# Two gate projections issued in the last attention job of a hybrid decoder layer, in place of jobs 8 to 10

## The chip, the core and the metric

The kernel runs on one NeuronCore of a Trainium2 chip. The core has five engines with an instruction stream each: TensorE (PE, matrix products into PSUM), VectorE (DVE), ScalarE (ACT), GpSimd (POOL) and SyncE (SP, which issues most DMA transfers). Each stream is worked off in its written order, and semaphores tie the streams together. The metric is the time of one execution on the device in microseconds (us), the median of the runs shown.

## The reference

One layer over 1024 tokens of width 1024. The normalised input is projected into four head groups of width 512, each of which also has a gate path; their outputs are normalised per head, gated, concatenated and projected back:

```python
h = rms_norm(h_res, norm_gain[l])
proj = h @ w_in[l]
(aq, ak, av, ag, bq, bk, bv, bg, cq, ck, cv, cg, cf, d_in, dg) = _split(proj, IN_WIDTHS)
...
oa = from_heads(differential_attention(qa, ka, va, bias_by_dist, lam))
...
ob = from_heads(stick_breaking_attention(...))
...
oc = from_heads(forgetting_attention(qc, kc, to_heads(cv, H_C, HEAD_DIM), log_f))
...
od = rwkv7_branch(d_in, rwkv_mu[l], ...)
mixed = jnp.concatenate([oa * jax.nn.silu(ag), ob * jax.nn.silu(bg),
                         oc * jax.nn.silu(cg), od * jax.nn.silu(dg)], axis=-1)
h_res = h_res + mixed @ w_out[l]
```

Group A is differential attention (4 heads), B stick-breaking attention (8 heads), C forgetting attention (8 heads), D an RWKV-7 state recurrence (8 heads). A gate here means silu of 128 columns of `ag`, `bg`, `cg` or `dg` for all tokens.

## The kernel before

The mixed width of 2048 is cut into 16 feature blocks f of 128: 0 to 3 are group A, 4 to 7 B, 8 to 11 C, 12 to 15 D. A projection (`proj`, L271) of 128 columns is 48 matmuls `pj` on L280: two token halves, eight slices of the contraction, three terms each (high and low parts of weights and activations). Its weights are loaded by two SP transfers and split by POOL into `wh` (L191) and `wl` (L192), 4 instructions. The activations `hTh` and `hTl` stay in SBUF until the last projection; `hp.close()` (L1143) gives their place to the tiles of the recurrence.

The attention runs as 12 jobs: 0 to 3 are pairs of heads of B, 4 to 7 heads of A, 8 to 11 pairs of heads of C. A job of C makes score tiles `sc` (L414, L418) on PE, a bias tile `bt` and a normalisation on POOL (L630, L631, L634), minima on DVE (L565), exponentials on ACT (L570); then `pv` (L426) transposes the weights (`pt`, L434), splits them into `pth` (ACT, L437) and `ptl` (DVE, L438) and multiplies them with the values (`po`, L443 and L444), four times 16 to 32 `po` rows for a job (8, 8, 16 and 16 pairs by halves and heads). While job i is in attention, the q, k and v projections of job i+1 are issued, and behind them the gate projections that the table `FILL` names for job i: `proj_gate_exp` (L397), whose evacuation of each half is a copy, three exponential or logarithm passes on ACT (L400, L402, L659, L660), one DVE (L658) and one POOL instruction (L404), and a store into `gates`. A scheduler places the instructions of each engine by priority and dependences; `hold` ties the first matmul of a gate that `FILL` names for job 11 behind that job's first score (L281).

A block f of `otb` or of a job is finished by `finish` (L456): loads of the attention output and the gate, a square on ACT (L294), a matmul `psn` of ones (L295) into a PSUM bank of one buffer, Ln and Exp on ACT (L238, L241), one DVE and one POOL product, and a store into `mix`. `FIN` names the blocks finished during a job, `LASTF` those finished behind the attention, after the two halves that job 11 has `held`.

Behind the last projection stands the recurrence of D, 16 chunks of 64 tokens: `chunk_local` and `chunk_state` (L991, L1018), each chunk six groups `psf` of matmuls (L986) with DVE steps between and a state step `pss` of 64 rows in the trace (L1040 to L1049); every second chunk is normalised (`pmean` L1063, `pvar` L1069). The output weights are split in 16 steps by `split_w` (L881): an SP load `wraw` into one of two buffers, a cast `woh` on ACT (L886, L891), a difference `wol` on POOL (L887, L892). The first eight use tiles that the attention frees, the other eight tiles that are free behind it. The output projection `pso` (L949) begins with three groups of feature blocks (4,5), (6,7), (8,9), runs then beside chunks of the recurrence, and takes blocks in the order of `WORDER`, (0,1), (10,11) and (2,3) next.

Of the kernel before, what the change touches and what calls it, by code (L numbers as in the profile page):

```python
# [41 lines left out]
SB = 1  # L42
EXP_LN_SET = 6
LATE_A = 4
FILL = {0: [4], 1: [5], 2: [6], 3: [7], 7: [8], 8: [9, 0, 1], 9: [10, 2], 10: [11, 3], 11: []}
FIN = {4: [4], 5: [5], 6: [6], 7: [7], 8: [0], 9: [1], 10: [2]}
OHW = 1152
NAV = 2
TMPB = 5
# [9 lines left out]
CUT2 = 4  # L59
EARLYG = 3  # L60
WFIRST = False
LASTF = (3,)


def shape_constants():
# [25 lines left out]
def hybrid_trunk_kernel(  # L91
# [296 lines left out]
    def proj_gate(f, tmp):  # L388
        def evac(hf, cs, ps):
            e = tmp.tile([P, HS], F32, tag="pjt", bufs=2, name="ge")  # L390
            sigmoid(e, ps)
            nc.vector.tensor_mul(e, ps, e)
            nc.sync.dma_start(gates[f, :, cs], e)

        proj(COL["abcd"[f // 4] + "g"] + f % 4 * P, evac)

    def proj_gate_exp(f, hold=None):  # L397
        def evac(hf, cs, ps):
            g = at.cbp.tile([P, HS], F32, tag="gg", bufs=2, name="gg")
            nc.scalar.copy(g, ps)  # L400
            e = at.cbp.tile([P, HS], F32, tag="ge", bufs=2, name="gx")
            nc.scalar.activation(e, g, AF.Exp, scale=-1.0)  # L402
            sigmoid_of(e)
            nc.gpsimd.tensor_mul(e, g, e)  # L404
            nc.sync.dma_start(gates[f, :, cs], e)

        proj(COL["abcd"[f // 4] + "g"] + f % 4 * P, evac, hold=hold)
# [48 lines left out]
    def finish(ot, f, J, sumw, width, tmp):  # L456
        cs = slice(J * HS, (J + 1) * HS)
        gt = at.fin.tile([P, HS], F32, tag="gl", bufs=2, name="gl")
        nc.sync.dma_start(gt, gates[f, :, cs])
        rs = head_rstd(ot, sumw, width, at.fin.tile([P, HS], F32, tag="tmp", bufs=TMPB, name="sq"), bank("av", 1, "psn"))  # L460
        y = at.fin.tile([P, HS], F32, tag="tmp", bufs=TMPB, name="y")
        nc.vector.scalar_tensor_tensor(y, ot, og[:, f:f + 1], rs, op0=ALU.mult, op1=ALU.mult)
        nc.gpsimd.tensor_mul(y, y, gt)
        nc.sync.dma_start(mix[f * P:f * P + P, cs], y)
# [79 lines left out]
    def proj_head_a(p, pl, tmp, late=None):  # L544
        t = qk_tiles(pl)
        proj_qk(COL["aq"] + p * P, "q", t, qkg[:, 0:1], tmp, late)
        proj_qk(COL["ak"] + p * P, "k", t, qkg[:, 1:2], tmp, late)
        t["v"] = proj_v(COL["av"] + p * P, pl, tmp, 1)
        tb = pl.tile([P, S], F32, tag="bt", bufs=2, name="tb")
        base = at.skew[p]  # L550
        src = bass.AP(base.tensor, base.offset + P - 1, [[OHW - 1, P], [1, S]])
        nc.sync.dma_start(tb, src)
        t["tb"] = tb
        return t
# [543 lines left out]
    with ExitStack() as st:  # L1098
# [9 lines left out]
        for i, (pf, af, j) in enumerate(jobs):  # L1108
# [6 lines left out]
            if i == 3:  # L1115
                late = []
                nxt = proj_head_a(0, pl, tmp, late)
                for f in FILL[i]:
                    proj_gate(f, tmp)
# [5 lines left out]
            if i < 3:  # L1125
                for f in FILL[i]:
                    proj_gate(f, tmp)
# [3 lines left out]
            elif i >= 7:  # L1131
                for f in FILL[i]:
                    proj_gate_exp(f, at.first if i in HOLD else None)
            for f in FIN.get(i, []):
                for J in range(2):
# [30 lines left out]
        for h in at.held:  # L1166
            finish(*h)
        for f in LASTF:
            for J in range(2):
# [42 lines left out]
```

## Time and profile before

| | |
|---|---|
| median of 3 runs | 1561.72 us (1561.05 to 1561.87) |
| the profiled execution | 1562.11 us, of which 1560.3 us are the span of its instructions |
| PE busy | 94% of the span, 8180 matmuls |
| DVE, ACT, POOL busy | 64%, 47%, 58% |
| granted TensorE clock | 0.984 of full speed |

The profile shows one execution. An engine's busy time is the time in which it had an instruction in work; a matmul's end is modelled and neighbours overlap in the pipeline, so a stream of matmuls that never pauses is priced by the step from one start to the next. The PE, PEld, DVE, ACT and POOL columns are busy times, with the number of instructions in brackets.

### The profile page before, as it was taken

The numbers are of one execution on the slowest core, as the hardware profiler recorded it, in microseconds if no ns is written. First come the engines' busy times: TensorE is split into PE (matmuls) and PEld (weight loads), VectorE is DVE, ScalarE is ACT, GpSimd is POOL, SyncE is SP. The second block draws the span as 40 slices with busy tenths as digits, with TensorE's granted clock in tenths as the row PEclk, the third lists the DMA queues.
The fourth block names the chain that finished last, engine by engine and source line by source line (L and its number), as shares of the span: only waits on it lengthen the run. The fifth ranks groups of instructions, "written<-read, shape, count | busy, mean of one in ns | idle before, by whom it ended". The sixth has DMA issues, their size and how long they took to land.

```text
span 1560.3 us, 23517 instructions
## 1 busy us (share of the span) xinstructions
PE 1465.9 (94%) x8180; PEld 1180.1 (76%) x8180; DVE 999.8 (64%) x1763; ACT 739.8 (47%) x1602; POOL 911.6 (58%) x999
## 2 busy tenths in 40 slices
PE   7899999988889898889999999999999999999998
PEld 4677777766667676668887878878877777888887
DVE  6677865488988877676677664463558774444321
ACT  5534343344444443475666665665566654211110
POOL 3566755899999999513334367767678745100000
PEclk9999999999999999989999999999999999999999
DMA  6444557321213131542233333324339547465231
GB/s 159 107 109 118 131 149 217 84 55 54 68 34 82 48 109 41 128 129 62 78 92 88 82 105 118 106 84 128 87 97 220 156 113 233 117 161 124 77 115 61
DMA packets 259759, 168.77 MB, mean 108 GB/s; under 512 B 127948, under 2 KB 222412, under 8 KB 259512
## 3 DMA queue, kind: packets, MB, share of 16 engines
q1 hardware_dynamic: 259640, 167.26, 40.1%
q8 instruction: 65, 1.06, 0.3%
q14 instruction: 54, 0.44, 0.1%
HBM read 107.40 MB, written 49.60 MB: 101 GB/s over the span
## 4 chain that ended last, share of the span: by engine, by line
PE 58%; POOL 20%; DVE 8%; issue 6%; ACT 3%; DMA 2%; SPq 1%; POOLq 0%; DVEq 0%; ACTq 0%
PE pj L280 25%; PE pso L949 10%; POOL yinv L874 7%; POOL ytmp L872 6%; PE psf L986 5%; POOL wl L192 3%; PE pt L434 3%; PE psn L295 3%; PE sc L414 2%; PE sc L418 2%; PE po L444 1%; PE po L443 1%; DMA wraw<-in_w_out_dram 1%; POOL wh L191 1%; POOL sh L699 1%
## 5 line engine op out<-in xcount | busy, mean ns | idle before, releaser
L280 PE MATMUL pj<-hTh,wh 128*128 128x512 f32 (+1 forms) x1040 | 423.2, 407 | 30.5 <-POOL wh L191 15.6
L280 PE MATMUL pj<-hTh,wl 128*128 128x512 f32 (+1 forms) x1040 | 417.9, 406 | 20.0 <-POOL wl L192 18.0
L280 PE MATMUL pj<-hTl,wh 128*128 128x512 f32 (+1 forms) x1040 | 416.1, 401 | 0.8 <-DVE hTl L268 0.8
L280 PEld LDWEIGHTS pj<-hTh,wh 128*128 128x128 f32 (+1 forms) x1040 | 199.0, 191 | 83.3 <-POOL wh L191 23.9
L280 PEld LDWEIGHTS pj<-hTh,wl 128*128 128x128 f32 (+1 forms) x1040 | 198.7, 191 | 70.8 <-POOL wl L192 24.5
L280 PEld LDWEIGHTS pj<-hTl,wh 128*128 128x128 f32 (+1 forms) x1040 | 198.8, 191 | 42.9 <-issue 3.0
L192 POOL TENSOR_TENSOR wl<-raw,wh 128x512 fp32r<-128x512 f32 (+1 forms) x130 | 183.4, 1411 | 8.4 <-PE pj L280 3.0
L191 POOL TENSOR_SCALAR wh<-raw 128x512 fp32r<-128x512 f32 (+1 forms) x130 | 99.1, 762 | 130.3 <-PE pj L280 106.3
L437 ACT CAST pth<-pt 128x512 fp32r<-128x512 f32 x240 | 107.9, 482 | 102.0 <-PE pt L434 96.4
L438 DVE TENSOR_TENSOR ptl<-pt,pth 128x512 fp32r<-128x512 f32 x240 | 125.4, 548 | 33.8 <-ACT pth L437 32.7
L492 DVE TENSOR_TENSOR_SCAN qs<-qs 128x128 f32<-128x128 f32 (+3 forms) x96 | 135.3, 1413 | 10.9 <-ACT qs L138 10.7
L570 ACT ACTIVATE Pt<-Pt,st 128x512 f32<-128x512 f32 (+2 forms) x192 | 117.0, 612 | 49.5 <-DVE st L565 45.2
L874 POOL TENSOR_TENSOR yinv<-yinv,ytmp 128x486 f32<-128x486 f32 (+44 forms) x106 | 129.6, 1222 | 4.1
L494 DVE TENSOR_TENSOR Pt<-Pt,qs 128x128 f32<-128x128 f32 (+3 forms) x96 | 102.3, 1068 | 38.7 <-POOL qs L491 17.1
L872 POOL TENSOR_TENSOR ytmp<-yinv 128x486 f32<-128x486 f32 (+44 forms) x106 | 117.7, 1111 | 8.1 <-DMA yinv<-mab 4.5
L1079 POOL TENSOR_TENSOR yc<-yc,lbg 128x512 f32<-128x512 f32 x16 | 20.8, 1298 | 164.6 <-DVE yc L1073 132.6
L434 PE MATMUL pt<-cst,Pt 128*128 128x128 f32 x720 | 115.0, 275 | 0.8 <-DVE Pt L494 0.5
L414 PE MATMUL sc<-k,q 128*128 128x512 f32 (+3 forms) x288 | 111.8, 389 | 3.7 <-DVE st L565 3.0
L434 PEld LDWEIGHTS pt<-cst,Pt 128*128 128x128 f32 x720 | 86.8, 141 | 17.7 <-issue 3.4
L418 PE MATMUL sc<-k,ql 128*128 128x512 f32 (+3 forms) x288 | 99.3, 349 | 0.0
L138 ACT ACTIVATE qs<-sc 128x128 f32<-128x128 f32 (+3 forms) x96 | 47.8, 498 | 89.9 <-DVE qs L492 42.5
L949 PE MATMUL pso<-wol,omh 128*128 128x512 f32 x224 | 89.1, 398 | 0.0
(255 smaller groups left out, 2961.7 us busy)
## 6 DMA issues: line engine op xcount, KB each, us to landing
raw<-in_w_in_dram SPq DMA_DIRECT2D x128, 256.0 KB, 3.0
cb<-cum SPq DMA_DIRECT2D x16, 512.0 KB, 4.2
bd<-abky SPq DMA_DIRECT2D x32, 256.0 KB, 4.9
wraw<-in_w_out_dram SPq DMA_DIRECT2D x16, 512.0 KB, 4.1
om<-mix SPq DMA_DIRECT2D x32, 256.0 KB, 3.1
q<-q SPq DMA_DIRECT2D x48, 128.0 KB, 2.3
k<-kl SPq DMA_DIRECT2D x48, 128.0 KB, 2.3
gl<-gates SPq DMA_DIRECT2D x24, 256.0 KB, 2.9
```

Of the source, the lines that this page charges most:

```text
L191: nc.gpsimd.tensor_scalar(wh[:, :, :M], raw[:, :, :M], 1.0, 0.0, op0=ALU.mult, op1=ALU.add)
L192: nc.gpsimd.tensor_sub(wl[:, :, :M], raw[:, :, :M], wh[:, :, :M].bitcast(F32))
L280: mm = nc.tensor.matmul(pss[hf][:M, :], lhsT=a[:, kt % 4, :M], rhs=b[:, kt, cs], start=n == 0, stop=n == 3 * KT - 1)
L414: mm = nc.tensor.matmul(ps[:, :w], lhsT=t[f"q{h}"][qh][:, qs], rhs=t[f"k{h}"][:, c0:c1], start=True, stop=False)
L418: nc.tensor.matmul(ps[:, :w], lhsT=t[f"l{h}"][qh][:, qs], rhs=t[f"k{h}"][:, c0:c1], start=False, stop=not diag)
L434: nc.tensor.transpose(pt[:, (b - a) * P:(b - a + 1) * P], ptiles[b][kb // 4][:, kb % 4 * P:(kb % 4 + 1) * P], ident)
L438: nc.vector.tensor_sub(pl[:, :n], pt[:, :n], ph[:, :n].bitcast(F32))
L492: nc.vector.tensor_tensor_scan(q[:, :w][:, ::-1], q[:, :w][:, ::-1], q[:, :w][:, ::-1], 1.0 if after is None else after, op0=ALU.mult, op1 ...
L570: nc.scalar.activation(et[:, :w], et[:, :w], AF.Exp, scale=-1.0, bias=init, accum_out=st[:, 2 + i:3 + i])
L872: nc.gpsimd.tensor_mul(t, y[:, a:a + n, r:r + 1].to_broadcast([P, n, r]), y[:, r:r + 1, :r].to_broadcast([P, n, r]))
L874: nc.gpsimd.tensor_add(y[:, a:a + n, :r], y[:, a:a + n, :r], t)
L949: mm = nc.tensor.matmul(ps[b][half], lhsT=l, rhs=r[half], start=n == 0, stop=n == 47)
```

## The change

Three tables are changed. Block 1 is projected as a gate in job 9 and no longer in job 8; blocks 2 and 3 move from jobs 9 and 10 to job 11, where `hold` puts them behind the first score. Block 2 is finished behind the attention, with block 3, and no longer in job 10.

```diff
-FILL = {0: [4], 1: [5], 2: [6], 3: [7], 7: [8], 8: [9, 0, 1], 9: [10, 2], 10: [11, 3], 11: []}
-FIN = {4: [4], 5: [5], 6: [6], 7: [7], 8: [0], 9: [1], 10: [2]}
+FILL = {0: [4], 1: [5], 2: [6], 3: [7], 7: [8], 8: [9, 0], 9: [10, 1], 10: [11], 11: [2, 3]}
+FIN = {4: [4], 5: [5], 6: [6], 7: [7], 8: [0], 9: [1]}
...
-LASTF = (3,)
+LASTF = (2, 3)
```

On PE, before the change, the rows around the first `po` of job 10 (bank `po_11055`, keys `k1_10558`); `pj_11906` is the second half of the last gate, block 3:

```order
L280 MATMUL pj_11906<-hTh_140,wh_11901 128x512
L280 MATMUL pj_11906<-hTl_141,wh_11901 128x512
L280 MATMUL pj_11906<-hTh_140,wl_11902 128x512
L443 MATMUL po_11055<-pth_11061,vs_10735 128x512
L444 MATMUL po_11055<-ptl_11062,vs_10735 128x512
L443 MATMUL po_11055<-pth_11071,vs_10735 128x384
L444 MATMUL po_11055<-ptl_11072,vs_10735 128x384
L443 MATMUL po_11055<-pth_11080,vs_10735 128x256
L444 MATMUL po_11055<-ptl_11081,vs_10735 128x256
```

With the change, the last scores of job 10 (keys `k1_10478`), its first long `po` bank, the first score of job 11 (keys `k0_11474`) and what follows; `pj_12347` is the first half of the gate of block 2:

```order
L414 MATMUL sc_11356<-k1_10478,q1_10476 128x512
L418 MATMUL sc_11356<-k1_10478,ql1_2400 128x512
L414 MATMUL sc_11361<-k1_10478,q1_10476 128x512
L418 MATMUL sc_11361<-k1_10478,ql1_2400 128x512
L443 MATMUL po_11204<-pth_11210,vs_10655 128x512
L444 MATMUL po_11204<-ptl_11211,vs_10655 128x512
L443 MATMUL po_11204<-pth_11221,vs_10655 128x512
L444 MATMUL po_11204<-ptl_11222,vs_10655 128x512
L414 MATMUL sc_11820<-k0_11474,q0_11470 128x128
L418 MATMUL sc_11820<-k0_11474,ql0_2396 128x128
L280 MATMUL pj_12347<-hTh_140,wh_12337 128x512
L280 MATMUL pj_12347<-hTl_141,wh_12337 128x512
```

Before, all projections are through when job 10's first `po` bank starts, and no matmul of a projection follows; now the first gate of the two begins some 80 rows behind the last matmul of block 11's gate, two thirds into job 10, and the rows between hold none. The first rows of the recurrence, which need the place of `hTh` and `hTl`, move behind the second gate.

On ACT, behind the attention, before the change: the casts of the last output weights (12 to 15), and the square (L294), Ln (L238) and Exp (L241) of the finishes; `psn_13088` and `psn_13100` belong to the first and second:

```order
L886 CAST woh12_14273<-wraw_14275 128x1024
L238 ACTIVATE sq_13087<-psn_13088,epst_129 128x512
L241 ACTIVATE sq_13087<-sq_13087 128x512
L294 ACTIVATE sq_13099<-ot_12186 128x512
L886 CAST woh13_14279<-wraw_14281 128x1024
L1011 COPY bdm0_12533<-psf_13251 64x4x64
L238 ACTIVATE sq_13099<-psn_13100,epst_129 128x512
L886 CAST woh14_14285<-wraw_14287 128x1024
```

The same place with the change; the first and second finish are `psn_13060` and `psn_13072`:

```order
L886 CAST woh12_14273<-wraw_14275 128x1024
L886 CAST woh13_14279<-wraw_14281 128x1024
L238 ACTIVATE sq_12887<-pvar_12889,epst_129 128x512
L241 ACTIVATE sq_12887<-sq_12887 128x512
L886 CAST woh14_14285<-wraw_14287 128x1024
L238 ACTIVATE sq_13059<-psn_13060,epst_129 128x512
L241 ACTIVATE sq_13059<-sq_13059 128x512
L886 CAST woh15_14291<-wraw_14293 128x1024
L294 ACTIVATE sq_13071<-ot_11998 128x512
L238 ACTIVATE sq_13071<-psn_13072,epst_129 128x512
```

The square of the second finish stood ahead of the cast of block 13 and stands now behind that of block 15, the last. Six finishes stand behind the attention and not four.

On PE, behind the attention with the change, the rows from the last of the first three output groups to the second finish; `pss_13191` is the state step of chunk 4, which before the change ran beside job 11's last `po` bank:

```order
L949 MATMUL pso_12966<-woh9_12946,oml_13030 128x512
L295 MATMUL psn_13060<-sq_13059,cst_65 128x512
L986 MATMUL psf_13144<-cR_12816,bd0_12503 128x128 x4
L986 MATMUL psf_13155<-rkv1_12513,bd1_12509 128x128 x4
L986 MATMUL psf_13162<-cR_12816,bdm0_12505 128x128 x4
L295 MATMUL psn_13072<-sq_13071,cst_65 128x512
L986 MATMUL psf_13168<-rkv1_12513,bd1_12509 128x128 x4
L986 MATMUL psf_13177<-cR_12816,bdm0_12505 128x128 x4
L986 MATMUL psf_13184<-rkv1_12513,bd1_12509 128x128 x4
L1040 MATMUL pss_13191<-cS_12880,cQ_13182 64x64
```

Everything behind the second `psn`, chunk 4 included, waits for it on PE; from the state step of chunk 7 on, the order of PE is that of before.

## Rows read from the trace of the kernel before

**Rows 1.** Busy time by stretch; after the engines: granted clock, DMA share, GB/s.

```profile
1069.20:1169.20 100.00, 99.18 (x481) 80.68 (x480) 51.10 (x122) 61.93 (x137) 69.49 (x88) 1.00 0.31 96
1169.20:1234.90 65.70, 60.43 (x438) 47.64 (x436) 53.76 (x135) 47.19 (x112) 56.89 (x72) 1.00 0.74 185
1234.90:1279.90 45.00, 43.07 (x380) 35.14 (x382) 35.46 (x78) 23.34 (x55) 20.18 (x20) 1.00 0.52 141
1279.90:1340.80 60.90, 58.18 (x456) 47.77 (x456) 30.23 (x42) 25.99 (x41) 29.43 (x15) 1.00 0.69 197
1340.80:1560.30 219.50, 215.46 (x1599) 182.01 (x1598) 75.69 (x132) 33.51 (x63) 13.09 (x10) 1.00 0.40 107
```

**Rows 2.** By stretch, the projections (L280) alone: PE, PEld, clock, DMA share, GB/s.

```profile
1069.20:1169.20 100.00, 72.64 (x289) 53.37 (x288) 1.00 0.31 96
```

**Rows 3.** By stretch, the recurrence's `psf` groups (L986) alone, same columns.

```profile
1169.20:1234.90 65.70, 21.66 (x160) 20.04 (x160) 1.00 0.74 185
1234.90:1279.90 45.00, 14.05 (x104) 13.00 (x104) 1.00 0.52 141
1279.90:1340.80 60.90, 19.01 (x144) 17.53 (x144) 1.00 0.69 197
```

**Rows 4.** Timeline of PE: start, duration; gate matmuls, finishes, recurrence.

```profile
1168.60 0.39 PE L280 MATMUL pj<-hTh,wh 128*128 128x512 f32 x1
1168.83 0.39 PE L280 MATMUL pj<-hTl,wh 128*128 128x512 f32 x1
...
1299.63 1.02 PE L295 MATMUL psn<-sq,cst 128*128 128x512 f32 x2
1300.49 1.05 PE L986 MATMUL psf<-cR,bdm 128*128 128x128 f32 x8
1301.38 1.06 PE L986 MATMUL psf<-rkv,bd 128*128 128x128 f32 x8
...
1303.32 1.02 PE L295 MATMUL psn<-sq,cst 128*128 128x512 f32 x2
...
1306.19 0.34 PE L1040 MATMUL pss<-cS,cQ 64*64 64x64 f32 x4
...
1308.25 1.16 PE L986 MATMUL psf<-cR,bd 128*128 128x128 f32 x8
...
1309.98 1.06 PE L295 MATMUL psn<-sq,ones 128*128 128x512 f32 x2
...
1315.47 1.12 PE L295 MATMUL psn<-sq,ones 128*128 128x512 f32 x2
```

**Rows 5.** POOL by line in 1069 to 1169 us: busy, mean ns; idle before.

```profile
L192 POOL TENSOR_TENSOR wl<-raw,wh 128x512 fp32r<-128x512 f32 x11 | 14.2, 1288 | 0.4
...
L404 POOL TENSOR_TENSOR gx<-gg,gx 128x512 f32<-128x512 f32 x6 | 8.2, 1364 | 4.4 <-ACT gx L660 4.4
...
L191 POOL TENSOR_SCALAR wh<-raw 128x512 fp32r<-128x512 f32 x11 | 7.2, 659 | 9.8 <-PE pj L280 9.8
```

**Rows 6.** Timeline of ACT behind the attention: casts of one weight buffer, two Ln.

```profile
1280.41 1.04 ACT L886 CAST wo<-wraw 128x1024 fp32r<-128x1024 f32 x1
...
1290.33 1.05 ACT L886 CAST woh<-wraw 128x1024 fp32r<-128x1024 f32 x1 [0.75 <-DMA wraw<-in_w_out_dram]
...
1304.63 1.05 ACT L886 CAST woh<-wraw 128x1024 fp32r<-128x1024 f32 x1 [1.73 <-DMA wraw<-in_w_out_dram]
...
1312.60 1.05 ACT L886 CAST woh<-wraw 128x1024 fp32r<-128x1024 f32 x1 [0.59 <-DMA wraw<-in_w_out_dram]
1313.55 0.68 ACT L238 ACTIVATE sq<-psn,epst 128x512 f32<-128x512 f32 x1
...
1317.26 0.68 ACT L238 ACTIVATE sq<-psn,epst 128x512 f32<-128x512 f32 x1
```

**Rows 7.** Busy time of all engines by stretch around a fall of the clock.

```profile
656.00:663.00 7.00, 3.75 (x21) 2.27 (x19) 1.91 (x3) 1.75 (x3) 1.88 (x2) 0.99 1.00 283
663.00:670.00 7.00, 4.34 (x11) 2.82 (x12) 2.91 (x5) 4.92 (x10) 0.00 (x0) 0.52 1.02 288
```

## The prediction

> **What bounds the kernel now.** I read the busy times by stretch first, then single lines within the stretches, then the timelines of PE and ACT. The stretches are cut at the first value product (`po`) of job 10 (1169.2 us) and of job 11 (1234.9), at the end of job 11's last one (1279.9, called E below), and at the state step of chunk 7 (1340.8), from which PE's order is the same in both kernels. In the 100 us between the first products of jobs 9 and 10 PE is busy 99%; behind them only 92%, while VectorE and GpSimd stand at 82% and 87% [rows 1]. The reader is to see that the first stretch is bound by PE and the second by the attention's chain through the other engines: the projections fill PE's pauses in the one, 289 matmuls of them, and in the other none are left [rows 2], only the recurrence's groups [rows 3].
>
> A busy PE is not yet a full one, so I price by steps from start to start where PE does not pause: 0.23 us for a 512-column matmul (0.227 in long series of 48), 0.111 per row of a `psf` group (0.89 for 8), 0.43 per row of a finish's `psn` (0.86 for 2), 0.032 per row of a state step (2.06 for 64) [rows 4]. Stretch one, called A, has 288 projection rows (65.4 us) and 16 `psn` rows (6.9), so the attention's own rows of a job cost about 27 and PE waits 1 us or so. B (65.7 us) has the same attention rows (27), 160 `psf` (17.8), 96 state rows (3.1), 8 `psn` rows and 4 of a normalisation (together 5.2): 53 of work, 12.7 of waits. C (45.0) has 36 score and 10 transpose rows fewer (18.7), 104 `psf` (11.5), 148 state rows (4.7), 1.8 for a normalisation: 36.7 of work, 8.3 of waits. D (60.9) has 126 output rows (28.6), 144 `psf` (16), 172 state rows (5.5), 5.2 of `psn` and normalisation: 55.3 of work, 5.6 of waits. Rows of one form are of several widths and the prices of the attention rows are a remainder, so each of these waits is an estimate good to some 2 us; they sum to 27.6.
>
> **The change part by part.** Counted in the order of PE between the same marks, A loses 96 projection rows (-21.8 us). B gains them and loses 144 `psf`, 96 state, 4 `psn`, 4 normalisation and 14 score rows: about -3.7. C gains 72 `psf`, 12 state and 14 score rows: +11. D gains 72 `psf`, 84 state rows, two `psn` and a normalisation: +14.2, and 7 output rows which the rest then lacks. No work is removed, so PE's sum is nil: the recurrence loses its place beside job 10, because its tiles need the room of the projections' inputs, and chunk 3's end and chunk 4 move behind E. Only the waits decide.
>
> *A, in future 78 us of work.* Its other engines lose two gates: on GpSimd 8 weight instructions of 0.66 and 1.29 us and 4 products of 1.36, 13.2 us [rows 5]. That leaves 56 us of its 69.5 for 78: 72%, against 87% in B. But behind block 11's gate stand some 80 rows without a projection, since the two gates are held behind job 11's first score, and that stands behind job 10's last. There PE follows the attention. At the least nothing is lost (1 us); at the most the job runs no faster than in B's mix and takes 88 (11 us). I take 3, since the bare part is about a sixth of the stretch.
>
> *B, 49 us of work.* The 96 rows lie in the middle as independent work. At the least 3 us of waits are left, at the most all 12.7. I take 6.5: the rows ahead of the gates and behind them are about 17 of 49, and at B's old share (12.7 of 53) they wait 4, the start of the recurrence and a few per cent of the filled part the rest. The 13.2 us on GpSimd, the eight exponential passes and the four stores of the gates come into this stretch and take the place of chunks 0 to 2's vector work.
>
> *C, 48 us.* Without filler, as before, and with all of the first weight splits in it. At the old share (8.3 of 36.7) it waits 11. Bounds 8 and 18: GpSimd gets the recurrence's clearing and the splits in one job instead of two.
>
> So job 11 ends after 81 + 55.5 + 59 = 195.5 us instead of 210.7: E comes some 15 us sooner.
>
> *D.* Behind E the splits of the last weights run in a loop of load, cast and difference over two buffers, which starts with a cast just behind E. In one buffer the casts come at 0.5, 10.4, 24.7 and 32.7 us from E (1280.41, 1290.33, 1304.63, 1312.60 against 1279.9; one left out) [rows 6]. Now ScalarE's order puts the square of the second finish behind that last cast: 32.7 + 1.05 + 0.6 puts its `psn` no sooner than E + 34.4; before, it began at E + 23.4 (1303.32) [rows 4]. PE's rows up to it are 72 output rows, 48 `psf`, 64 state, a normalisation and a `psn`, 26.3 us: PE stands 8 us, and chunk 4 with it. Then come four finishes in series, 3.7 us each by the two Ln (1313.55, 1317.26) [rows 6] or 5.5 by the two last `psn` (1309.98, 1315.47) [rows 4], so 15 to 22 us beside some 15 of PE's work; what follows waits for their stores as before. D waits 9 to 17; I take 12.5, nearer the lower price, as no cast stands between these finishes. Late next is chunk 5 and the output group (0,1).
>
> The waits are then 3 + 6.5 + 11 + 12.5 = 33 against 27.6: **+5.4 us**. The profiled execution took 1562.11, of which 1560.3 were span; the median of the runs is 1561.72, 0.4 less. From it: 1567.1, say **1567**.
>
> **The rivals.** *Faster: the two regimes fill each other.* With filler in B and shorter A, PE waits 1, 3 and 8 in A to C and the finishes keep to 9: 21 against 27.6, -6.6, so 1555, and down to 1551 if the end of the attention moves further. For it speaks that GpSimd has room in A (72%); against it, that the finish cannot start before the last cast [rows 6]. It decides if E comes more than 20 us sooner. The Trainium skill, Perfetto Trace Analysis, section Optimization Strategy, says that where the most contended engine changes over time, interleaving such regimes may improve performance; by that rule this case would be the outcome.
>
> *No change to be told.* A measurement of this kernel can tell about 0.2%, 3.1 us. Waits of 25 to 30 give 1559 to 1564.5: the gain up to E, 18 or so, and the longer D cancel.
>
> *Much slower: job 10 cannot be run in 80 us.* If its scores keep B's pace, A waits 11, and B fills less: 42 to 44, so 1576 to 1578. Against it speaks the 72%.
>
> *Slower by the clock.* In 656 to 663 us PE was busy 3.75 of 7 us, and in the next 7 the granted clock was 0.52, so nearly all at 1.2 GHz in place of 2.4 [rows 7]. In the stand behind E, PE has three groups (2.7 us) in 11 us. Should the clock fall for as long, some 5 us of PE's rows take twice their time, of which the finishes hide half: +2.5 on the forecast, 1569.5. The Trainium skill, TensorE: Matmul & The Clock Gate, section HAM oscillation, warns that waits between bursts of matmuls put PE back at half clock; by that rule this case adds to the forecast. No fall is seen between 1069 and 1560 us, where the granted clock is 1.00 [rows 1].
>
> **How the numbers follow.** Forecast, +3.1 to +9: 0.40. No change: 0.22. Faster: 0.18. Much slower: 0.14. Clock: 0.06. Slower by over 0.2% is 0.60, within it 0.22, faster 0.18. The range leaves out about a tenth on each side: below 1556 the lower part of the faster case, above 1577 the upper part of the much slower one. The likeliest case's own range is 1565 to 1571.
>
> **What would show it.** Job 10's first product some 81 us behind job 9's, and job 11's last one near 1265 us, would bear out A to C; a span from there to chunk 7's state step near 82 us, with PE idle some 8 us ahead of the second `psn` and waiting for ScalarE, would bear out D. The prediction is wrong if E comes at 1255 or sooner, if the weight casts run faster than 7.4 us a buffer, or if E does not come sooner at all.

## The result, and the profile after

The changed kernel takes 1584.28 us (median of four, 1582.63 to 1585.45) where the kernel before takes 1561.8: ratio 1.0142, 95% interval 1.013 to 1.0155. It is slower by 22.5 us, far more than the 0.2% that can be told; the forecast was 1567 with a range from 1556 to 1577. The sign was right, the size was not.

The profiled execution took 1582.63 us, of which 1580.8 were span, 20.5 more than before. The same marks as in the prediction lie at 1070.6 us (job 9's first value product), 1155.8 (job 10's), 1219.3 (job 11's), 1278.2 (E, the end of job 11's last) and 1363.0 (chunk 7's state step). The first view is the busy times by stretch, with A and B cut once more: at the last row of block 11's gate (1144.2), and at the first and the last row of the two moved gates (1172.2, 1201.4).

```profile
1070.60:1144.20 73.60, 72.83 (x364) 59.37 (x363) 41.53 (x107) 46.12 (x109) 49.64 (x68) 1.00 0.32 94
1144.20:1155.80 11.60, 6.73 (x22) 2.89 (x21) 5.67 (x12) 8.50 (x17) 11.60 (x14) 0.90 0.47 154
1155.80:1172.20 16.40, 14.23 (x62) 11.23 (x63) 10.81 (x30) 10.18 (x26) 8.04 (x12) 0.76 0.29 101
1172.20:1201.40 29.20, 29.20 (x150) 24.62 (x149) 12.82 (x39) 17.22 (x41) 20.62 (x29) 1.00 0.17 64
1201.40:1219.30 17.90, 13.90 (x62) 10.11 (x60) 11.68 (x23) 10.41 (x22) 15.39 (x17) 0.81 1.04 251
1219.30:1278.20 58.90, 54.08 (x481) 45.62 (x480) 46.52 (x105) 33.04 (x80) 35.46 (x39) 1.00 0.51 132
1278.20:1363.00 84.80, 76.26 (x627) 62.41 (x626) 41.86 (x62) 33.79 (x55) 34.78 (x19) 0.96 0.70 190
1363.00:1580.80 217.80, 213.85 (x1592) 180.87 (x1591) 75.94 (x133) 33.52 (x63) 13.05 (x10) 1.00 0.40 107
```

The columns are those of [rows 1]. Read the second, third and fifth row: in 45.9 us TensorE runs 146 rows, in the 29.2 us of the moved gates alone it runs 150. These three stretches, called bare below, hold attention and finish rows alone, but for the recurrence's first 16 `psf` rows at the end of the last. Added up, A took 85.2 us (forecast 81), B 63.5 (55.5), C 58.9 (59), D 84.8 (82). E was to come 15 us sooner behind job 9's first product; it came 3.1 sooner (207.6 us against 210.7), and only 1.7 from the span's start. The granted clock, 1.00 everywhere behind 1069 us before the change, is below it in just these three stretches and in D.

What TensorE waited for in the first two of them (waits by releaser, 1144.2 to 1172.2; us in total, times, longest):

```profile
PE psn L295 <- ACT sq L294: 3.0, 1, 3.0
PE pt L434 <- DVE ptl L438: 2.1, 2, 1.3
PE sc L414 <- DVE st L565: 1.1, 2, 0.9
PE po L443 <- ACT sq L238: 0.8, 1, 0.8
```

These are the attention's own steps and the finishes' (L294, L238), one behind the other, with nothing independent in TensorE's order to put between them. This view holds only waits in which TensorE stood idle; late operands and a lower clock also lengthen the steps of a TensorE that shows as busy. So these stretches are also priced row by row at the step from start to start that the same kind of row takes in the kernel before where TensorE does not pause (0.43 us for a `psn` row, 0.109 for a row of `pt`, 0.23 for 512 columns): 4.9 us of work in the 11.6, 9.7 in the 16.4, 9.1 in the 17.9, and 28.9 in the 29.2 of the gates. By this estimate, good to some half us each, the three bare stretches wait 22.2 of 45.9 us, 48%, what the lower clock costs included; the gates' stretch waits 1%. (A job of C has 48 `po` rows in the trace, in banks of 8, 8, 16 and 16. The 8, 8, 16 and 16 given for the kernel before are rows and not pairs.)

### The profile page after: what moved, and what is told of

It is laid out like the page before. It is cut to its first block, busy times and chain, and to the rows that moved or that the text cites. A ratio compares the mean times of both kernels' runs of the same rounds, so it can differ in the third digit from the quotient of the medians.

```text
span 1580.8 us, 23501 instructions
## 1 busy us (share of the span) xinstructions
PE 1466.7 (93%) x8180; PEld 1180.7 (75%) x8180; DVE 1001.6 (63%) x1763; ACT 740.5 (47%) x1602; POOL 910.8 (58%) x999
## 4 chain that ended last, share of the span: by engine, by line
PE 59%; POOL 20%; DVE 9%; issue 6%; ACT 4%; DMA 2%; SPq 1%; POOLq 0%; DVEq 0%; ACTq 0%
PE pj L280 25%; PE pso L949 10%; POOL yinv L874 6%; POOL ytmp L872 6%; PE psf L986 5%; POOL wl L192 3%; PE psn L295 3%; PE pt L434 3%; PE sc L414 2%; PE sc L418 2%; PE po L444 1%; PE po L443 1%; DVE qs L492 1%; DMA wraw<-in_w_out_dram 1%; POOL wh L191 1%
## 5 line engine op out<-in xcount | busy, mean ns | idle before, releaser
L280 PE MATMUL pj<-hTh,wh 128*128 128x512 f32 (+1 forms) x1040 | 421.4, 405 | 30.7 <-POOL wh L191 15.2
L280 PE MATMUL pj<-hTh,wl 128*128 128x512 f32 (+1 forms) x1040 | 414.8, 403 | 20.0 <-POOL wl L192 17.4
L280 PE MATMUL pj<-hTl,wh 128*128 128x512 f32 (+1 forms) x1040 | 414.8, 399 | 0.9 <-DVE hTl L268 0.9
L280 PEld LDWEIGHTS pj<-hTh,wh 128*128 128x128 f32 (+1 forms) x1040 | 198.1, 190 | 82.2 <-POOL wh L191 21.6
L280 PEld LDWEIGHTS pj<-hTh,wl 128*128 128x128 f32 (+1 forms) x1040 | 197.5, 190 | 70.3 <-POOL wl L192 24.3
L280 PEld LDWEIGHTS pj<-hTl,wh 128*128 128x128 f32 (+1 forms) x1040 | 197.6, 190 | 41.9 <-issue 2.6
L434 PEld LDWEIGHTS pt<-cst,Pt 128*128 128x128 f32 x720 | 88.2, 143 | 23.1 <-DVE ptl L438 7.1
```

The lines of the kernel that those rows point to most:

```text
L280: mm = nc.tensor.matmul(pss[hf][:M, :], lhsT=a[:, kt % 4, :M], rhs=b[:, kt, cs], start=n == 0, stop=n == 3 * KT - 1)
L434: nc.tensor.transpose(pt[:, (b - a) * P:(b - a + 1) * P], ptiles[b][kb // 4][:, kb % 4 * P:(kb % 4 + 1) * P], ident)
```

## The experiments

All times are medians; differences are to the kernel before, timed on the same chip; where a run is compared with the changed kernel the two were timed apart, and the kernel before differed by up to 0.6 us between such timings. Theory 1 grew out of the view above: the loss is that of stretches of attention rows with neither a projection nor a recurrence group among them, and of the two finishes behind E. "Rows" are TensorE's.

**No hold.**

```diff
-HOLD = (11,)
+HOLD = ()
```

> The changed kernel without the hold: blocks 2 and 3 are still in job 11's list, but their first matmul need not stand behind job 11's first score, so their 96 rows come right behind block 11's gate. Theory 1 (the rows without a projection lose the time, by PE's waits and by the granted clock that falls behind them): the stretch from 1145 to 1172 us, in which the changed kernel's PE fell 20 us behind its own work, is filled; some 10 us of that come back as waits in job 11, which is then without filler from its first third on. The end of job 11 comes 8 to 12 us sooner, 1572 to 1576. Theory 2 (the attention's chain on VectorE, GpSimd and ScalarE sets the pace of jobs 10 and 11 whatever PE does in its pauses): the end of job 11 within 3 us, 1581 to 1587.

1571.89 us, ratio 1.0061 (1.0046 to 1.0076): 12.4 less than the changed kernel, theory 1 (0.1 under its range). Its busy times by stretch, cut at job 9's first product, block 11's last gate row, block 3's last, job 11's first product, E and chunk 7:

```profile
1069.60:1143.00 73.40, 72.61 (x363) 59.17 (x362) 42.10 (x107) 45.87 (x109) 49.43 (x68) 1.00 0.33 94
1143.00:1171.90 28.90, 28.90 (x134) 23.13 (x133) 11.65 (x23) 18.13 (x34) 20.82 (x22) 1.00 0.37 119
1171.90:1226.70 54.80, 47.88 (x374) 40.96 (x373) 46.92 (x115) 37.47 (x94) 46.73 (x63) 0.94 0.72 174
1226.70:1269.90 43.20, 41.33 (x365) 34.62 (x364) 33.51 (x78) 26.84 (x61) 23.65 (x26) 1.00 0.47 123
1269.90:1350.40 80.50, 69.50 (x519) 56.03 (x517) 41.24 (x56) 30.70 (x50) 34.27 (x19) 0.96 0.70 188
```

The 28.9 us behind block 11's gate now hold 134 rows in place of 84 in 28.0, the projections end 29.5 us sooner, and E comes 8.3 us sooner. D keeps 80.5.

**Rows that only fill.** Behind block 11's gate, into projection banks that nothing reads:

```diff
+                mm = nc.tensor.matmul(ps[:, k * P:(k + 1) * P], lhsT=ident, rhs=cst[:, :P], start=True, stop=True)
+                after(mm, first)
...
+                idle_rows(DUM.get(i, 0))
```

> The changed kernel with 48 further products of the identity with itself (128x128, f32, into projection banks that nothing reads) behind block 11's gate, where PE stood 4.9 of 11 us (1145 to 1156). They load no other engine. At 0.111 us each they are 5.3 us of PE's work that the output does not need. Theory 1 with the clock: PE stays busy there, the fall of the clock from 1153.4 to 1160.3 us does not come, and what it cost (at most half of the 6 us in which PE was busy in it, 3 us) comes back: 1579 to 1583 in spite of the added work. Theory 2 (the clock costs nothing there, as PE is not what is waited for): no gain, and the added rows that do not fit into the pauses are paid: 1584 to 1589.

1585.72 us, ratio 1.0149 (1.0132 to 1.0166): 1.4 more than the changed kernel. By the number that is theory 2, but I had mis-sized the edit: a 128x128 product in f32 shows as two rows, so the 48 are 96, and 10.7 us of work instead of 5.3. Most of that found room. TensorE is busy and the clock full where both had sagged (first row: last row of block 11's gate to job 10's first product; second: to the first row of the moved gates):

```profile
1142.30:1157.30 15.00, 15.00 (x112) 13.12 (x110) 6.61 (x13) 9.35 (x18) 12.18 (x14) 1.00 0.49 151
1157.30:1173.50 16.20, 12.34 (x72) 9.06 (x72) 11.16 (x32) 10.75 (x27) 8.49 (x13) 1.00 0.22 73
```

The first stretch holds 88 of the added rows, 9.8 us, and takes 15.0 us where it took 11.8 (1144.0 to 1155.8): two thirds of them cost no time. The second holds the other eight (0.9 us) and takes 16.2 us at a clock of 1.00; in the changed kernel it took 16.4 at 0.76. So the fall of the clock there cost at most some 1.1 us, an estimate that gives the eight rows their full price. The pauses hold room for further rows; what is missing is rows that the output needs. The bare stretch at 0.81 has no such counterpart.

**Finishes written ahead of the seventh early weight split.**

```diff
         for n, (f, spot) in enumerate(zip(WORDER, spots)):
+            if n == MID:
+                mid()
```

> The changed kernel with the six finishes behind job 11 written ahead of the seventh of the eight early weight splits instead of behind the eighth, so that ScalarE's order has the second finish's square two casts sooner or more. Theory 1 (the stand ahead of the second sum, 1304 to 1312, is ScalarE's order: its square stood behind the last weight cast): the stretch from the end of job 11 to chunk 7's state step shrinks from 84.7 us by 6 to 10, and the whole to 1574 to 1578. Theory 2 (the finishes' length in series or the loads of the weights bound this stretch, and the square's place does not matter): less than 2 us, 1582 to 1586.

1585.31 us, ratio 1.0149 (1.0134 to 1.0164): no gain. The second sum came 5.8 us behind E, but the first output row 43.9 in place of 2.1: finishes and output rows share the rotating buffers `gl` and `tmp`, so the output rows now stood behind the finishes. D was 88.2. The edit moved more than the square, and decides nothing about it.

**Late finishes alone, in the kernel before.**

```diff
-... 8: [0], 9: [1], 10: [2]}
+... 8: [0], 9: [1]}
-LASTF = (3,)
+LASTF = (2, 3)
```

> The kernel before with one part of the change alone: the two finishes of block 2 move from job 10's list to those behind job 11; the gates stay where they were. Theory 1 (two more finishes in series behind the end of job 11 cost 3.7 to 5.5 us each, of which PE's own work there hides part; the two normalisations and squares that leave jobs 10 and 11 give back 1 to 2): 1565 to 1570. Theory 2 (the finishes are hidden behind output rows and recurrence groups as long as the recurrence is not late): 1560 to 1563.

1569.06 us, ratio 1.004 (1.0025 to 1.0055): +6.7, theory 1. In the profile, which is of the shortest of four executions (1567.07), D was 70.7 against 60.9, the jobs ahead 4.0 shorter.

**Hold on block 3 alone**, then **the same with block 2's finishes as before**, then **block 3 alone moved and held**, finishes as before. The first is an edit of the changed kernel, the second and third of the kernel before, of which the new `FILL` is shown:

```diff
+                    proj_gate_exp(f, at.first if i in HOLD and f == 3 else None)
...
+FILL = {... 8: [9, 0], 9: [10, 1], 10: [11, 2], 11: [3]}
...
+FILL = {... 8: [9, 0, 1], 9: [10, 2], 10: [11], 11: [3]}
```

> The changed kernel with the hold on block 3 alone: block 2's first matmul is free and its 48 rows come right behind block 11's gate, block 3's stay in job 11 behind its first score. Theory 1 (each stretch of attention rows without anything independent loses time, so the two gates are worth most when each covers one): the stretch from job 9's first product to the end of job 11 is 196 to 201 us (207.6 changed, 200.3 with no hold), the whole 1568 to 1572. Theory 2 (the waits only change places, and what counted in the run without the hold was the earlier start of the recurrence): block 3 delays that start as both did, the stretch 204 to 207, the whole 1577 to 1582.

> The same order of the gates (block 2 in job 10's list and free, block 3 held in job 11), but with the finishes of block 2 left in job 10's list and only those of block 3 behind job 11, as in the kernel before. Theory 1 (two more finishes behind the end of job 11 cost 6.7 us by themselves, as the run with the late finishes alone showed): 5 to 8 us less than the run with the hold on block 3 alone, 1561 to 1566. Theory 2 (with the recurrence later by a chunk the output rows and the weights' loads set the stretch behind job 11, and the number of finishes matters little): less than 3 us between the two.

> The kernel before with block 3 alone moved from job 10's list to job 11's, held behind its first score; all the rest, the finishes too, as before. Theory 1: job 10 keeps block 11 and the jobs ahead keep their three gates, so a stretch of some 40 rows of job 10 stays bare; the recurrence starts one gate later: 1562 to 1568. Theory 2 (any gate that is held behind job 11's first score costs half of what two do, 6 us, and the finishes cost nothing here): 1568 to 1573.

1578.19 us, ratio 1.0105 (1.008 to 1.0131); 1573.58, 1.0072 (1.0057 to 1.0087); 1579.71, 1.0111 (1.0091 to 1.0131). The first is theory 2's (its stretch to the end of job 11 was 205.1 us, in a profile of the longest of its four executions, 1583.94): one gate in each bare stretch is worth 6.1 us, half of the 12.4 of both gates free, while the later of them still holds the recurrence back. The second is 4.6 below it, between the two theories, and its time missed theory 1's. The third missed both: one held gate, finishes untouched, costs 17.4 us. That turned me from the gates to what stands behind them: the recurrence, whose tiles take the room of the projections' inputs, started at 1211.4 in it (its profile, too, is of the longest execution, 1582.93), against 1179.3 before (first `psf` row). The room shows in the traces: GpSimd begins to clear the recurrence's first tile `bd` 0.1 to 1.0 us behind the end of the last projection row in every kernel here. That row ended at 1169.4 us before and at 1201.8 with the change, and the clearing is, before and with the change:

```profile
1169.57 1.95 POOL L969 MEMSET bd<- 128x2048 f32 x1 [1.16 <-PE pj L280]
1202.68 1.80 POOL L969 MEMSET bd<- 128x2048 f32 x1
```

**Casts of weights 14 and 15 behind the second finish's square.**

```diff
+            if f in LASTC:
+                after(cast, at.sqs[SQN])
```

> The changed kernel with the casts of the last two weights (14 and 15) ordered on ScalarE behind the square of the second finish, which stood behind them at 1311.1. Theory 1 (the square's place behind the last cast makes the stand ahead of the second sum): the second sum comes 6 to 9 us sooner behind the end of job 11 than 34.4 us, and the stretch to chunk 7's state step is 76 to 80 us instead of 84.8; the whole 1575 to 1579. Theory 2 (the second finish waits for buffers and the normalisation of chunk 3, which itself waits behind an earlier cast whose weight has not landed): less than 3 us, 1581 to 1586.

1584.26 us, ratio 1.0141 (1.0124 to 1.0158): theory 2. The square came 5 us sooner (1306.1), the second sum 32.5 us behind E in place of 34.4, D was 82.8. So the square's place alone was not what made the stretch long.

**No hold, and block 2's finishes as before**: blocks 11, 2 and 3 in job 10's list.

```diff
-... 8: [9, 0, 1], 9: [10, 2], 10: [11, 3], 11: []}
+... 8: [9, 0], 9: [10, 1], 10: [11, 2, 3], 11: []}
```

> Gates dealt out as in the changed kernel up to block 1 (two in job 8's list, two in job 9's), but blocks 11, 2 and 3 all in job 10's list with no hold, and the finishes as in the kernel before (block 2's in job 10's list, only block 3's behind job 11). Theory 1 (what the change costs is the rows left without a projection, and the two late finishes): neither is there, 1562 to 1567, that is the run without the hold less the 6.7 us of the late finishes. Theory 2 (the later finish of the gates by a few us and their weights' and products' place beside job 10's end cost by themselves): 1568 to 1573.

1562.85 us, ratio 1.0006 (0.9997 to 1.0015): the kernel before, theory 1. Two gates may move a job further on for nothing, as long as nothing stands bare and the finishes stay.

**The recurrence held, the gates untouched**, in the kernel before:

```diff
+                ...; at.fpo = at.fpo or mm
...
+            if rw.s is None and q == 0: after(mm, at.fpo)
```

> The kernel before with its gates and finishes untouched, and the recurrence's first groups held on TensorE behind job 11's first value product, where the changed kernel has them too; from 1169 us to there job 10 and job 11 run with neither a projection nor a recurrence group. Theory 1 (it is the recurrence that is missing as filler beside the attention; the gates' own work on the other engines in job 11 is harmless): job 11's first product comes only 7 to 12 us sooner than 65.7 us behind job 10's although 21 us of PE's work has left, the stretch from the end of job 11 to chunk 7's state step is 75 to 82 us, the whole 1574 to 1582. Theory 2 (the gates' exponentials, products and stores in job 11 slow its chain, and the recurrence may come late at the price of the longer last stretch alone): 1564 to 1569.

1580.3 us, ratio 1.0116 (1.0101 to 1.0131): +18.2 with no gate moved, theory 1. Busy times, cut at job 10's and job 11's first product, E and chunk 7:

```profile
1068.40:1168.40 100.00, 99.18 (x482) 80.74 (x481) 51.05 (x122) 62.00 (x137) 69.48 (x88) 1.00 0.32 96
1168.40:1221.80 53.40, 38.59 (x173) 24.66 (x172) 37.11 (x98) 39.10 (x92) 49.07 (x61) 0.94 0.69 185
1221.80:1267.50 45.70, 45.39 (x387) 39.29 (x385) 36.73 (x88) 27.46 (x66) 25.52 (x30) 1.00 0.46 110
1267.50:1356.80 89.30, 81.65 (x719) 68.03 (x718) 41.66 (x66) 30.46 (x51) 31.84 (x17) 0.96 0.68 177
```

The second row is B without a recurrence group: 173 rows in 53.4 us, against 438 in 65.7 before [rows 1]. Priced row by row as above it holds 27.7 us of work, so it waits 25.7, 48%, the share of the changed kernel's bare stretches. The time is in theory 1's range, but its parts are not: job 11's first product came 12.3 us sooner than before, just beyond the 7 to 12 expected, and D took 89.3, 7.3 more than the 75 to 82. The profile is of the shortest of four executions, 1577.56.

**Gates sooner**, the kernel before with block 11 in job 9's list:

```diff
-... 9: [10, 2], 10: [11, 3], 11: []}
+... 9: [10, 2, 11], 10: [3], 11: []}
```

> The other direction: the kernel before with block 11 moved from job 10's list to job 9's. Theory 1: PE was 99% busy beside job 9 and nothing is bare there, so no stretch gains or loses filler: 1559 to 1564. Theory 2 (the end follows the last projection and the recurrence's start, and the sooner these come, the sooner the end): the last projection some 5 us sooner, 1555 to 1559.

1569.27 us, ratio 1.0044 (1.0028 to 1.006): both theories missed. The last projection did not come sooner (1171.6 us). What moved is the recurrence's order: chunk 4's state step stands 16.9 us ahead of E, before 1.9. B and C together took 14.0 us longer and what follows E only 7.7 less. Why these groups cost more beside the attention than behind it was not tried.

**Chunk 3's normalisation ahead of five weight casts**, in the changed kernel:

```diff
+            cast = nc.scalar.copy(wh[0], raw); f in LASTC and after(cast, rw.norms[1])
...
+LASTC = (3, 12, 13, 14, 15)
```

> The changed kernel with five weight casts (3, 12, 13, 14, 15) ordered on ScalarE behind the logarithm of chunk 3's normalisation, which waited at 1303.9 behind a cast whose weight had not landed, though its sum was there at 1298; PE's stand from 1305.8 to 1310.7 was released by VectorE, which had that normalisation ahead of the recurrence's next step. Theory 1 (this normalisation, which stands behind the end of job 11 only since the recurrence is late, makes the stand and not the second finish's square): the stand shrinks, the stretch to chunk 7's state step is 76 to 81 us instead of 84.8, the whole 1575 to 1580. Theory 2 (the weights' loads and the six finishes in series set that stretch, and what is taken from the stand comes back behind the casts, which come later): less than 3 us, 1581 to 1587.

1577.81 us, ratio 1.01 (1.0085 to 1.0115): 6.5 less than the changed kernel, theory 1; D was 78.3. First the changed kernel's timelines of TensorE, ScalarE and VectorE around the stand behind E, then the same rows of TensorE and ScalarE in this run:

```profile
1304.64 1.16 PE L986 MATMUL psf<-rkv,bd 128*128 128x128 f32 x8 [0.69 <-ACT sq L238]
1310.69 2.07 PE L986 MATMUL psf<-cR,bdm 128*128 128x128 f32 x8 [4.89 <-DVE cR L1022]
1312.56 1.68 PE L295 MATMUL psn<-sq,cst 128*128 128x512 f32 x2
1314.07 1.05 PE L986 MATMUL psf<-rkv,bd 128*128 128x128 f32 x8
...
1302.95 1.04 ACT L886 CAST woh<-wraw 128x1024 fp32r<-128x1024 f32 x1 [3.37 <-DMA wraw<-in_w_out_dram]
1303.90 0.68 ACT L238 ACTIVATE sq<-pvar,epst 128x512 f32<-128x512 f32 x1
1310.17 1.05 ACT L886 CAST woh<-wraw 128x1024 fp32r<-128x1024 f32 x1 [2.26 <-DMA wraw<-in_w_out_dram]
1311.12 0.63 ACT L294 ACTIVATE sq<-ot 128x512 f32<-128x512 f32 x1
...
1305.28 1.70 DVE L1071 TENSOR_TENSOR yc<-yc,sq 128x512 f32<-128x512 f32 x1 [12.89 <-ACT sq L241]
1307.02 3.02 DVE L1073 TENSOR_SCALAR yc<-yc,lg,lb 128x128 f32<-128x128 f32 x4
1309.96 0.68 DVE L1022 TENSOR_TENSOR cR<-psf,cR 128x512 f32<-128x512 f32 x1
```

```profile
1301.65 1.06 PE L986 MATMUL psf<-rkv,bd 128*128 128x128 f32 x8
1304.72 1.16 PE L986 MATMUL psf<-cR,bdm 128*128 128x128 f32 x8 [2.02 <-DVE cR L1022]
1305.72 1.02 PE L295 MATMUL psn<-sq,cst 128*128 128x512 f32 x2
...
1296.68 0.69 ACT L238 ACTIVATE sq<-pvar,epst 128x512 f32<-128x512 f32 x1 [5.41 <-PE pvar L1069]
1302.21 0.61 ACT L294 ACTIVATE sq<-ot 128x512 f32<-128x512 f32 x1
1305.92 1.04 ACT L886 CAST woh<-wraw 128x1024 fp32r<-128x1024 f32 x1 [3.10 <-DMA wraw<-in_w_out_dram]
```

In the changed kernel a cast whose weight had not landed (ScalarE stood 3.37 us for its DMA) kept the normalisation's logarithm until 1303.9; VectorE then did the normalisation (1305.28 to 1309.96) ahead of the recurrence's next step L1022, and TensorE stood 4.89 us for that step. With the logarithm ahead of the casts it stands 2.02 us. The row order had it: the second sum stood behind that group on TensorE too. Not all of D's 6.5 us is this stand: 2.5 us are eleven output rows that now come behind chunk 7's state step, and row by row D's waits fell from 14.0 to 10.0 us. Some 1.6 us of these were the clock, by the changed kernel's lines: in the stand it fell to 1.2 GHz (granted 0.51 from 1306.9 to 1313.5 us), and the group and the sum behind it took 1.87 and 1.51 us to the next start, where they take 0.89 and 0.86 at 2.4 GHz [rows 4]. In this run the granted clock is 1.00 over D.

## Why the prediction was wrong, step by step

**The step that failed** is the wait of the rows ahead of the gates and behind them. I had "about 17 of 49" us of work there, "at B's old share (12.7 of 53) they wait 4", and in A "I take 3, since the bare part is about a sixth of the stretch". The work was nearly right (9.7 + 9.1 us); they waited 15.5, and A's bare end waited 6.7. B's old share came from a stretch whose pauses the recurrence filled, 160 `psf` and 96 state rows of 438 ([rows 1, 3]). Without it, and without a projection, the same attention waits about half of the time, as the run with the held recurrence shows with no gate moved (25.7 of 53.4). The share of a filled stretch was put on an unfilled one, and B's upper bound of 12.7, taken from the same stretch, was none.

By the prediction's own prices of work the waits are then A 7.2 (forecast 3), B 14.5 (6.5), C 10.9 (11), D 15.3 (12.5): 14.9 us more than forecast, beside the 15.1 by which the profiled 1582.63 passes its own 1562.11 + 5.4. (1.6 us of D's are the seven output rows, which it counted but did not price and which the rest lacks; 1.4 us came ahead of A.) With the row prices above on both kernels the waits grew by 7.2 us in A, 1.2 in B, 2.8 in C and 8.3 in D, where the forecast's own terms were +2.0, -6.2, +2.7 and +6.9. So A's bare end was priced too low by some 5 us and the gain that B was to bring, 6, was none.

**What held.** No work is removed, and the rest behind chunk 7 is 217.8 us against 219.5, by the seven output rows that went into D. The filled part of B waits next to nothing. C came to a tenth of a us, closer than an estimate good to 2 us can claim; C has the recurrence as filler in both kernels, so there the old share could be carried. The second finish's sum came at E + 34.4, as forecast.

**What held in size but not in cause.** D's sum point was right to the tenth, but not for the reason given, the square behind the last cast: with the square ahead of the cast it came at E + 32.5 and the time did not change; with chunk 3's normalisation ahead of five casts it came at E + 29.3 and 6.5 us were gained. So the agreement of the sum's time was luck. The casts behind their loads do hold a part of the stretch, through a normalisation that stands behind E because the recurrence is late.

**The rivals.** The much slower case gave 1576 to 1578 and came nearest, but by another way: A waited 7.2 and not 11, and the gates did fill B's middle. "The two regimes fill each other" needed E 20 us sooner and got 3.1: the move left a stretch ahead of the gates and one behind them with neither regime's filler. By the rule of the Trainium skill, Perfetto Trace Analysis, section Optimization Strategy, that goes with it (interleaving regimes may improve performance), this was the case to expect; the trace does not agree here, as the kernel became slower. The clock fell in more places than its rival named: the granted clock is 0.90, 0.76 and 0.81 in the bare stretches and 0.96 over D, where TensorE stood idle 2.2 to 4.9 us of 11.6 to 17.9 and in D 8.5 of 84.8. The Trainium skill, TensorE: Matmul & The Clock Gate, section HAM oscillation, warns of just that, and the trace agrees. In the stretch where it could be compared the fall of the clock cost at most 1.1 us of 16.4, and in D some 1.6 by the rows; in the other two bare stretches its cost was not tried apart.

**The accounts.** Times against the first recurrence row (`psf`) in the profile of each kernel:

```
finishes as before        first psf   time      two finishes late   first psf   time
before                     1179.3    1561.8     late finishes        1177.5    1569.1
no hold, finishes          1186.8    1562.9     no hold              1187.3    1571.9
block 3 held, finishes     1203.6    1573.6     hold on block 3      1206.8    1578.2
block 3 alone moved        1211.4    1579.7     changed kernel       1217.0    1584.3
recurrence held            1222.6    1580.3
```

Some 7.5 us of delay cost nothing that can be told; beyond, the time grows with the delay, by half a us for each over the whole left column (17.4 us for the 35.8 behind 1186.8), but unevenly (0.6 us in its last 11.2). The rows differ in more than the delay, so this is no price of the delay by itself. Late finishes come on top. The change is a recurrence that starts 37.7 us later (18.2 us for 43.3 in the run that delays it alone) and two late finishes (6.7 alone): 24.9 by their sum, 22.5 measured. But the parts do not add stretch by stretch. The waits by the row prices, in us, estimates good to about 1:

```
                     A      B      C      D
before              1.8   14.6    9.1    5.7
recurrence held     1.8   25.7    4.7   14.5
late finishes       2.0   13.8    9.3   14.9
changed kernel      9.0   15.8   11.9   14.0
```

Behind E the late recurrence alone and the late finishes alone each add some 9 us, and both together no more, so how D's loss is shared between them stays open. Ahead of E the changed kernel loses most in A, whose end has no projection any more; in B the gates only replace what the recurrence filled before. The run with the gates sooner (1180.7, 1569.3) stands outside this table. No version here beats the kernel before.

## What to carry to other kernels

Before a filler is moved, list what remains in each stretch as independent work for the bound engine, and take the wait of a stretch only from a stretch with the same filler; a share read where something else filled the pauses says nothing about the bare chain. When work is held back, ask what its buffers block: here a large part of the gates' price was the start of the recurrence that needed the room of the projections' inputs. And where an in-order engine has work that waits for loads, look at everything behind it, not only at the one instruction that the change puts there.

## What the runs showed of the hardware that I had not expected

TensorE's clock fell to 1.2 GHz for parts of the bare rows and of D. The first of these falls came as TensorE had just stood 3.04 us, the one in D 1 us into a stand of 4.89 (the changed kernel):

```profile
1154.00:1160.00 6.00, 5.22 (x18) 3.86 (x17) 2.35 (x6) 2.83 (x6) 3.83 (x4) 0.50 0.61 208
1306.90:1313.50 6.60, 2.81 (x10) 2.29 (x11) 6.29 (x9) 2.55 (x4) 5.59 (x4) 0.51 0.90 195
```

In the stretch that can be compared it hardly mattered: it took 16.4 us at a granted 0.76, and 16.2 at 1.00 (2.4 GHz throughout) with 0.9 us of rows more in it. TensorE stood idle 2.2 us of the one and 3.9 of the other: what the slower rows took longer was for the most part pause at full clock.

Some of the variants vary more from run to run than the kernel before does: the one with the hold on block 3 alone took 1574.4 to 1583.9 us in four runs, the kernel before 1560.6 to 1564.8 beside it.
